# A four-layer decoder trunk: order edges behind the newest weight parts, read-backs used two stages later, and smaller pieces of side work

## The chip, the cores and the metric

The kernel runs on one core of one Trainium2 chip. Times are device microseconds (us) of a run of the whole program; lower is better. On the core, TensorE (PE) multiplies, ScalarE (ACT), VectorE (DVE) and GpSimd (POOL) work on rows, and SyncE (SP) issues transfers. Each engine works through its own instructions in order. POOL, SP and, twice, ACT also issue DMA transfers.

## What is computed

A decoder trunk with 256 positions, width 2048 and four layers in fp32. The layers' mixers are latent attention (MLA), sparse attention with an indexer and top-k (DSA), sliding-window attention with sinks, and latent attention again. Each layer also attends to a memory of 256 rows with four heads, and gates all heads. Cut to what matters:

```python
def reference(x, mem, ...):
    mem_n = _rmsnorm(mem, mem_norm)
    for i in range(DEPTH):                       # 4
        h = _rmsnorm(x, norm_in[i])
        self_out, mq, gate = <mixer i>(h, ...)   # h @ w_in, then attention: 2048 wide
        mem_out = _memory_attention(mq, mem_n @ w_mem_kv[i])      # 1024 wide
        y = jnp.concatenate([self_out, mem_out], axis=-1) * jax.nn.silu(gate)
        x = x + y @ w_out[i]
    return _rmsnorm(x, final_norm)
```

## The kernel before

**The stream of weights.** Nearly all arithmetic is activations times weights, and every weight is read once. SP loads a stage of weights, two slices of 128 rows by 512 columns (512 KB, tile `wr`, WR = 4 buffers, `stage`). fp32 is kept by splitting each number into two parts of a shorter type (fp32r): per slice, `parts_of` lets ACT copy `wr` to its high part `wh` (through `copy_act`, L75) and DVE subtract to get the low part `wl` (L84); each has WS = 4 buffers. `rows_by` (L381) then issues six matmuls of 128x512 per slice: for two halves of the positions, high by high, high by low and low by high. One slice with its copy, its subtraction and its six matmuls is called a *weight step* here. The results are `acc_q`, `acc_g` (the gate), `acc_mq` (queries to the memory), `acc_wo` (the output projection) and so on.

**Read-backs.** A result of `rows_by` has positions on partitions, and the next product needs features there. DVE turns it in blocks of 32 (`turn_blocks`, L284; tiles `et` and `th`), POOL writes that to DRAM (`put`, L299, `turned<-et`) and reads it back in the other layout with four transfers (`get`, L306, `fq<-turned`, `pT<-turned` and so on). That is a read-back. The tiles are `fa` (features of the low-rank queries, made into `cT` with a gain), `fq` (queries), `kn` (keys), `pT` (softmax weights), `gT` (the gate). Their consumers are: `row_parts` (the parts of fq, one 128x1024 copy on ACT and one subtraction on DVE), `exact_parts` (the same for kn and pT), in the grouped layers (DSA, window) the copies `qS<-fq`, in the latent layers `qrT<-fq` (rotary), `gained` for cT.

**Jobs and ticks.** `rows_by` calls `other_work` once per stage, that is every two weight steps; this is a *tick*. `after(n, job)` runs a job n ticks on. `features` puts a read-back's `get` BACK = 3 ticks behind its `put`, and its use USE = 9 ticks behind it. So the softmaxes (`weights`), the products with the values (`weighted`: `mo` L765, `o` L629 and L1197) and the gated outputs (`gated` L581, `write` L1207: DVE multiplies o with gT into `yt`, ACT and DVE split it into the parts of `y`) are written into the code between weight steps.

**What sets the order.** The code's order is not the last word: a scheduler puts each engine's instructions in an order by a timing model of its own, unless they are pinned (`keep_in_program_order`) or depend on each other. Weights loads are not pinned as a whole, so a consumer of a read-back can be placed earlier or later among the weight parts than it was written.

**Parts of a layer.** A layer's work runs in parts, in the order memory 0, self 0 to 3, memory 1: each part makes its queries, its gate and its attention, and while the next part's input products run, its `y` is finished; then `w_out` multiplies it (`acc_wo` reads `y`). `Part.finish` runs ticks without weights until y is written. In a grouped part `weights` runs as four jobs, two ticks apart, each with 4 quarter softmaxes, and `bm` (position biases, L1100) is loaded by POOL at the start of the part into a buffer that an earlier part holds. One `memset` per job (L1164) is POOL's.

**The last layer.** While it runs, `split_ahead` (L1332 to L1346) prepares the last part's output weights: POOL loads a piece of 128x256 into `hl` (2 buffers), ACT and DVE split it, and POOL writes it to DRAM (`sw`), so that the end can run without splitting. 16 pieces, ten half ticks each.

Of the kernel before, what the change touches and what calls it, by code (L numbers as in the profile page):

```python
# [15 lines left out]
P = 128  # L16
S = 256
# [10 lines left out]
PQ, AUX, WR, WS, PT, WARM = 3, 4, 4, 4, 4, 11  # L28
BACK, USE = 3, 9
# [17 lines left out]
def kernel(ctx: ExitStack, tc: tile.TileContext, a: dict, out: bass.AP,  # L47
# [23 lines left out]
    def part_tile(dt=F32R):  # L71
        return wk.tile([P, 512], dt, name="hl", tag="hl", bufs=2)
# [7 lines left out]
    pinned = []  # L80

    def split(hi, lo, src):
        copy_act(hi, src)
        nc.vector.tensor_sub(lo, src, f32(hi))  # L84

# [207 lines left out]
    def put(ets, d=None):  # L293

        u, n = len(ets), ets[0].shape[-1] // 4
        if d is None:
            d = dr.tile([u, 4, 32, 4, n], F32, name="turned", tag=f"turned{u * n}", bufs=6)
        for t, et in enumerate(ets):
            nc.gpsimd.dma_start(d[t].rearrange("i p j n -> (i p) (j n)"), et)  # L299
        return d  # L300

    def get(dst, d, pin=None):

        n = d.shape[-1]
        for j in range(4):
            inst = nc.gpsimd.dma_start(dst[32 * j:32 * j + 32].rearrange("p (i n) -> p i n", n=n),  # L306
                                       d[:, :, :, j, :].rearrange("t i p n -> p (t i) n"))
            if pin is not None:
                pin(inst)
# [21 lines left out]
    def gained(dst, gcol, n=4):  # L331

        def use(t):
            for m in range(n):
# [3 lines left out]
                copy_act(hi, src, scale=g)  # L338
                nc.vector.scalar_tensor_tensor(lo, src, g, f32(hi), op0=OP.mult, op1=OP.subtract)
        return use  # L340

    def row_parts(t):
# [4 lines left out]
        copy_act(h4, src)  # L347
        nc.vector.tensor_sub(l4, src, f32(h4))
        return hi, lo

    def exact_parts(hi, lo):

        copy_act(hi, f32(lo))
        nc.vector.tensor_sub(lo, f32(lo), f32(hi))

    def parts_of(wr, c0, n):
        wh = wp.tile([P, 512], F32R, name="wh", tag="wh", bufs=WS)
        wl = wp.tile([P, 512], F32R, name="wl", tag="wl", bufs=WS)
        split(wh[:, :n], wl[:, :n], wr[:, c0:c0 + n])
        return wh, wl  # L360

    def rows_by(xt, kts, w, k0, cols, name, prepare=None, each=None, exact_first=False):
# [4 lines left out]
        for s in range(0, kts, ST):  # L367
# [3 lines left out]
            for k in range(m):  # L371
# [7 lines left out]
                for n_, (t, v, w_) in enumerate(seq):  # L379
                    later = [z for z in seq[n_ + 1:] if z[0] == t]  # L380
                    nc.tensor.matmul(acc[t][:, :n], q[:, v, (s + k) % 4, t * P:(t + 1) * P], w_[:, :n],  # L381
                                     start=s + k == 0 and v == 0 and w_ is wh,
                                     stop=s + k == kts - 1 and not later)
# [195 lines left out]
    def gated(y, o, gT, j):  # L579
        yt = tmp("yt")  # L580
        nc.vector.tensor_mul(yt.rearrange("p (m u c) -> p m u c", m=2, c=32),  # L581
                             o.rearrange("p (m u c) -> p m u c", m=2, c=32),
                             gT[:, :, j:j + 2, :].rearrange("p u m c -> p m u c"))
        y3 = yt.rearrange("p (a b) -> p a b", a=2)
        split(y[:, 0, j:j + 2, :], y[:, 1, j:j + 2, :], y3)
# [40 lines left out]
    def attend(o, v, pT):  # L626

        for n_, (l, r_) in enumerate(((v[0], pT[0]), (v[0], pT[1]), (v[1], pT[0]))):
            nc.tensor.matmul(o, l, r_, start=n_ == 0, stop=False)  # L629
# [59 lines left out]
    class Memory(Part):  # L689
        def __init__(self, nm, i, w, mq0, g0, part, behind):  # L690
# [8 lines left out]
            def keys():  # L699
# [6 lines left out]
                get(flat_of(self.k[:, 1]), mk[i][part], pin)  # L706
                after(USE - BACK, lambda: exact_parts(self.k[:, 0], self.k[:, 1]))
# [3 lines left out]
            def queries(t):  # L711
                self.q = row_parts(t)
                for h in range(2):
                    after(1 + 2 * h, lambda h=h: self.weights(h))
# [3 lines left out]
        def weights(self, h):  # L718
# [4 lines left out]
            for b in range(2):  # L723
# [3 lines left out]
                for m in (2 * h, 2 * h + 1):  # L727
                    qh, ql = (z[:, m, b * P:(b + 1) * P] for z in self.q)
                    for l, r in ((qh, k[:, 0, :, m, :]), (qh, k[:, 1, :, m, :]), (ql, k[:, 0, :, m, :])):
                        nc.tensor.matmul(sp[:, :S], l, r, start=n_ == 0, stop=n_ == 5)  # L730
# [17 lines left out]
            def back():  # L748
                pL = weights_tile()[:, :512]
                get(f32(pL), d)  # L750
                after(USE - BACK, lambda: self.weighted(h, pL))
            after(BACK, back)

        def weighted(self, h, pL):
# [5 lines left out]
            for j in range(2):  # L760
# [3 lines left out]
                for n_, (l, r_) in enumerate(seq):  # L764
                    nc.tensor.matmul(o[:, j * S:(j + 1) * S], l, r_, start=n_ == 0, stop=n_ == 5)  # L765
# [17 lines left out]
    class Latent:  # L783
# [62 lines left out]
        def rotary(self, g):  # L846
# [9 lines left out]
            def use(zs):  # L856
                self.qr = [act.tile([P, 4, S], F32R, name="qrT", tag="aux", bufs=AUX) for z in range(2)]
                for z in range(2):
                    for h, main, low in ((0, slice(0, 64), slice(64, P)), (1, slice(64, P), slice(0, 64))):
# [3 lines left out]
                        copy_act(hi, src)  # L863
                        nc.vector.tensor_sub(lo, src, f32(hi))  # L864
# [5 lines left out]
    class LatentPart(Part):  # L870
# [30 lines left out]
        def weights(self, h):  # L901
            k, kr, qr = self.k, self.of.kr, self.of.qr[self.g % 2]

            def score(b):
# [8 lines left out]
                for n_, (l, r_) in enumerate(seq):  # L913
                    nc.tensor.matmul(sp[:, :S], l, r_, start=n_ == 0, stop=n_ == len(seq) - 1)  # L914
# [3 lines left out]
            def back():  # L918
                pT = weights_tile()
                get(f32(pT)[:, :384], d)  # L920
                after(USE - BACK, lambda: self.weighted(h, pT))
# [15 lines left out]
    class Grouped:  # L937
# [39 lines left out]
        def dup(self, dst, src, n):  # L977

            s3 = src.rearrange("p (g d) -> p g d", g=n)
            for g0 in range(0, n, 2):  # L980
                m = min(2, n - g0)
                hl = part_tile()[:].rearrange("p (g v e d) -> p g v e d", g=2, v=2, e=2)
# [108 lines left out]
    class GroupedPart(Part):  # L1091
        def __init__(self, of, g):
            super().__init__()
            self.of, self.g, nm = of, g, of.nm
            self.bm = bm = act.tile([P, 8, S], F32, name="bm", tag="big3")
            tab = tabs[0 if of.sparse else 1][g]
            for v in range(2):
                for e in range(2):
                    at = 64 * v + 32 * e
                    nc.gpsimd.dma_start(  # L1100
                        bm[at:at + 32, :4],
                        bass.AP(tensor=tab.tensor,
                                offset=tab.offset + 4 * e * N_TAB + 63 + 32 * v * (8 * N_TAB - 1),
                                ap=[[8 * N_TAB - 1, 32], [N_TAB, 4], [1, S]]))
# [7 lines left out]
            def queries(t):  # L1112
                self.q = [act.tile([P, 2, 8, 2, 32], F32R, name="qS", tag="pq", bufs=PQ) for z in range(2)]
                for z in range(2):
                    for h, main, low in ((0, slice(0, 64), slice(64, P)), (1, slice(64, P), slice(0, 64))):
                        hi, lo = (self.q[z][rows, h].rearrange("p u j c -> p u (j c)") for rows in (main, low))
                        src = t[main, :, 2 * z:2 * z + 2, :].rearrange("p u j c -> p u (j c)")
                        copy_act(hi, src)
                        nc.vector.tensor_sub(lo, src, f32(hi))
# [4 lines left out]
                for n in range(4):  # L1124
                    after(1 + 2 * n, lambda n=n: self.weights(n // 2, n % 2))
# [3 lines left out]
        def weights(self, half, odd):  # L1129
            of, g, bm, q = self.of, self.g, self.bm, self.q  # L1130

            def score(r, k0, n):
                sp = misc("sp")
                qb = q[half][:, odd, 2 * r:2 * r + 2].rearrange("p v j c -> p (v j c)")
                nc.tensor.matmul(sp[:, :2 * n], qb, of.k[:, g, :, k0:k0 + n], start=True, stop=True)
# [17 lines left out]
            if of.sparse:  # L1153
                e2, e1 = bm[:, 4 + half * 2 + odd, :], ring(P)
                quarter_softmax(score, bias, ((0, 0, e2[:, 192:]), (1, 0, e1)), None)
                turn_blocks(et, 0, e1)
# [4 lines left out]
            else:  # L1161
                nsk = nsink[:, u0:u0 + 1]
                e0, e1 = ring(P), ring(P)
                nc.gpsimd.memset(e0[:, 64:], 0.0)  # L1164
                quarter_softmax(score, bias, ((0, 0, e0[:, :64]), (1, 0, e1)), nsk)
                turn_blocks(et, 0, e0)
                turn_blocks(et, 1, e1)
# [5 lines left out]
            def back():  # L1173
# [3 lines left out]
                if len(self.pTs) == 4:  # L1177
                    after(USE - BACK, self.weighted)
# [269 lines left out]
```

## Time and profile before

| | |
|---|---|
| median of 3 runs | 2557.74 us (2557.07 to 2557.97) |
| the profiled execution | 2558.04 us |
| its span (first to last instruction) | 2556.1 us |
| granted TensorE clock, mean over the span | 0.992 |
| busy time of PE, DVE, ACT, POOL | 2498.3, 1853.7, 1520.6, 569.1 us |

The page gives each engine's busy time, then groups of instructions by line and tile with their count, busy time, mean in ns, and the idle time of the engine just before them with what ended it ("24.9 <-DMA fq<-turned 24.8": 24.8 us of 24.9 ended when the read-back into fq landed). The list of waits gives, for an engine and what released it, total us, number and longest. The windows view gives for each stretch of time the length, then busy time and count for PE, PEld, DVE, ACT and POOL, then the granted clock (1 is full speed), the DMA share and GB/s.

### The profile page before, as it was taken

How to read it: one execution, taken by the hardware profiler on the slowest of the kernel's cores; microseconds unless marked ns; L12 is line 12 of the kernel's file. 1: busy time of each engine (PE TensorE's matmuls, PEld its weight loads, DVE VectorE, ACT ScalarE, POOL GpSimd, SP SyncE). 2: the span in 40 equal slices, each digit the busy share in tenths (PEclk: the TensorE clock that was granted, in tenths of full speed). 3: DMA queues.
4: the chain of work that ended last, by engine and by line, in shares of the span. 5: the costliest groups of instructions: out<-in, count | busy, mean ns of one | idle time of the engine just before them, and what ended most of it. 6: DMA issues, size and time to landing. Idle time of an engine off the chain costs nothing. (4 is left out here: it accounts for less than half of the span.)

```text
span 2556.1 us, 37640 instructions
## 1 busy us (share of the span) xinstructions
PE 2498.3 (98%) x11766; PEld 2070.6 (81%) x11766; DVE 1853.7 (73%) x3840; ACT 1520.6 (59%) x3107; POOL 569.1 (22%) x1078
## 2 busy tenths in 40 slices
PE   9999999999999999999999999999999999999998
PEld 7888887787787889887878788878779778888887
DVE  6556555676776687887887776888867567777677
ACT  6555555565565557665666565666656555566564
POOL 3000001133222310123322112222320123432240
PEclk9999999999999999999999999999999999999999
DMA  8787767898879776778878677877875789997994
GB/s 283 250 267 236 235 213 227 233 259 238 228 233 264 236 243 203 222 225 255 276 234 246 200 222 245 253 246 246 245 238 173 224 248 278 267 263 225 269 313 148
DMA packets 404633, 613.96 MB, mean 240 GB/s; under 512 B 80881, under 2 KB 182641, under 8 KB 403793
## 3 DMA queue, kind: packets, MB, share of 16 engines
q1 hardware_dynamic: 347360, 449.71, 58.4%
q0 software_dynamic: 56352, 160.87, 20.3%
q8 instruction: 93, 1.52, 0.2%
q14 instruction: 108, 0.88, 0.1%
q10 hardware_dynamic: 720, 0.98, 0.1%
HBM read 535.83 MB, written 81.89 MB: 242 GB/s over the span
## 5 line engine op out<-in xcount | busy, mean ns | idle before, releaser
L75 ACT ACTIVATE wh<-wr 128x512 fp32r<-128x512 f32 (+1 forms) x1712 | 1046.5, 620 | 774.5 <-DVE wl L84 308.4
L84 DVE TENSOR_TENSOR wl<-wr,wh 128x512 fp32r<-128x512 f32 (+1 forms) x1712 | 1137.8, 676 | 482.7 <-ACT wh L75 473.2
L381 PE MATMUL acc_g<-wh,xT 128*128 128x512 f32 x1536 | 490.6, 394 | 5.3 <-ACT wh L75 5.3
L381 PE MATMUL acc_wo<-wh,y 128*128 128x512 f32 x1504 | 478.5, 393 | 3.6 <-ACT wh L75 3.4
L381 PEld LDWEIGHTS acc_g<-wh,xT 128*128 128x128 f32 x1536 | 290.7, 189 | 67.3 <-ACT wh L75 9.2
L381 PEld LDWEIGHTS acc_wo<-wh,y 128*128 128x128 f32 x1504 | 283.9, 189 | 62.5 <-ACT wh L75 5.6
L381 PE MATMUL acc_g<-wl,xT 128*128 128x512 f32 x768 | 304.6, 397 | 9.1 <-DVE wl L84 8.8
L381 PE MATMUL acc_wo<-wl,y 128*128 128x512 f32 x752 | 296.3, 394 | 2.2 <-DVE wl L84 2.0
L306 POOL DMA_DIRECT2D pT<-turned x320 | 175.0, 554 | 254.2 <-DMA turned<-et 43.1
L299 POOL DMA_DIRECT2D turned<-et x136 | 76.0, 559 | 549.7 <-DVE et L284 482.0
L381 PEld LDWEIGHTS acc_g<-wl,xT 128*128 128x128 f32 x768 | 145.4, 189 | 45.2 <-DVE wl L84 16.1
L381 PEld LDWEIGHTS acc_wo<-wl,y 128*128 128x128 f32 x752 | 142.2, 189 | 32.1 <-DVE wl L84 4.8
L381 PE MATMUL acc_mq<-wh,xT 128*128 128x512 f32 x512 | 162.6, 391 | 0.0
L381 PE MATMUL acc_mk<-wh,mT 128*128 128x512 f32 x512 | 160.4, 392 | 2.2 <-ACT wh L75 2.2
L381 PE MATMUL acc_q<-wh,xT 128*128 128x512 f32 x512 | 159.9, 390 | 0.0
L381 PE MATMUL acc_mv<-wh,mT 128*128 128x512 f32 x512 | 156.4, 389 | 0.9 <-ACT wh L75 0.9
L381 PE MATMUL acc_cq<-wh,xT 128*128 128x512 f32 x384 | 123.9, 402 | 6.4 <-ACT wh L75 6.4
L381 PE MATMUL acc_qn<-wh,cT 128*128 128x512 f32 x384 | 121.4, 392 | 3.5 <-ACT wh L75 3.2
L1367 DVE TENSOR_TENSOR xc<-xc,acc_wo 128x1024 f32<-128x1024 f32 x92 | 111.8, 1215 | 9.0 <-PE acc_wo L381 8.7
L381 PEld LDWEIGHTS acc_mk<-wh,mT 128*128 128x128 f32 x512 | 96.8, 189 | 22.8 <-ACT wh L75 2.6
L381 PEld LDWEIGHTS acc_mv<-wh,mT 128*128 128x128 f32 x512 | 96.0, 188 | 21.1 <-ACT wh L75 1.0
L381 PEld LDWEIGHTS acc_mq<-wh,xT 128*128 128x128 f32 x512 | 96.1, 188 | 19.8 <-ACT wh L75 0.7
(313 smaller groups left out, 3914.4 us busy)
## 6 DMA issues: line engine op xcount, KB each, us to landing
wr<-in_w_out_dram SPq DMA_DIRECT2D x188, 512.0 KB, 4.6
wr<-in_w_in_a_dram SPq DMA_DIRECT2D x176, 512.0 KB, 5.1
wr<-in_w_mem_kv_dram SPq DMA_DIRECT2D x125, 512.0 KB, 4.7
wr<-in_w_in_b_dram SPq DMA_DIRECT2D x116, 512.0 KB, 5.1
wr<-in_w_in_c_dram SPq DMA_DIRECT2D x104, 512.0 KB, 5.1
wr<-in_w_uq_dram SPq DMA_DIRECT2D x144, 256.0 KB, 5.3
turned<-et POOLq DMA_DIRECT2D x104, 256.0 KB, 4.4
wr<-in_w_ukv_dram SPq DMA_DIRECT2D x64, 256.0 KB, 6.0
```

Of the source, the lines that this page charges most:

```text
L75: inst = nc.scalar.activation(o, i, AF.Copy, scale=scale)
L84: nc.vector.tensor_sub(lo, src, f32(hi))
L299: nc.gpsimd.dma_start(d[t].rearrange("i p j n -> (i p) (j n)"), et)
L306: inst = nc.gpsimd.dma_start(dst[32 * j:32 * j + 32].rearrange("p (i n) -> p i n", n=n), d[:, :, :, j, :].rearrange("t i p n -> p (t i) n"))
L381: nc.tensor.matmul(acc[t][:, :n], q[:, v, (s + k) % 4, t * P:(t + 1) * P], w_[:, :n], start=s + k == 0 and v == 0 and w_ is wh, stop=s + k ...
L1367: nc.vector.tensor_add(xs, xs, acc)
```

## The change

It does nine things. No arithmetic is left out and none is added.

1. **Edges.** `weight_op` remembers per engine the newest weight part (ACT, DVE), the newest last matmul of a weight step (PE) and the newest `put` (POOL). `late` adds an edge without a semaphore from it to an instruction: the scheduler may not place that instruction ahead of it on its engine. `late` is applied to the consumers of read-backs (cT, fq, qS, qrT, kn, pT), to the first matmul of each score and of each product with values, to `yt` and the parts of y, and to the gets on POOL.
2. **Ticks.** BACK 3 to 4, USE 9 to 11; a new WAIT = 11 for the softmax weights; the memory's keys are still split 6 ticks behind their read, which USE - BACK no longer gives.
3. **WR** 4 to 5.
4. **Halves.** `row_parts` and the `qS` copies run in two halves, one tick apart; fq's copies become 128x512.
5. **Softmaxes** of a grouped part in eight jobs, one tick apart, in place of four. In a memory part 0 the second pair of heads is two ticks behind the first, in part 1 one tick.
6. **bm** is loaded 11 ticks later (`biases`).
7. **The memset** of e0 goes from POOL to DVE.
8. **`dup`** takes its tile `hl` from the ring of `tmp`.
9. **`split_ahead`** runs 32 pieces of 128x128 in place of 16 of 128x256, five half ticks each, through two buffers of half the size.

The diff, cut to its core:

```diff
-PQ, AUX, WR, WS, PT, WARM = 3, 4, 4, 4, 4, 11
-BACK, USE = 3, 9
+PQ, AUX, WR, WS, PT, WARM = 3, 4, 5, 4, 4, 11
+BACK, USE, WAIT = 4, 11, 11
...
+    newest = {}
+    def weight_op(inst):
+        newest[inst.ins.engine] = inst.ins
+    def late(inst):
+        behind = newest.get(inst.ins.engine)
+        if behind is not None:
+            tc.add_manual_dep(inst.ins, behind.name,
+                              mybir.DependencyInfo(mybir.DependencyClass.NoSync, mybir.DependencyReason.DATA),
+                              reason="behind the newest weights")
+    def late_copy(o, i, scale=1.0):
+        late(nc.scalar.activation(o, i, AF.Copy, scale=scale))
+    def late_split(hi, lo, src):
+        late_copy(hi, src)
+        late(nc.vector.tensor_sub(lo, src, f32(hi)))
...
     def put(ets, d=None):
-            nc.gpsimd.dma_start(d[t].rearrange("i p j n -> (i p) (j n)"), et)
+            weight_op(nc.gpsimd.dma_start(d[t].rearrange("i p j n -> (i p) (j n)"), et))
-    def get(dst, d, pin=None):
+    def get(dst, d):
-            if pin is not None:
-                pin(inst)
+            late(inst)
...
     def row_parts(t):
-        copy_act(h4, src)
-        nc.vector.tensor_sub(l4, src, f32(h4))
+        def half(m):
+            late_split(h4[:, m:m + 2], l4[:, m:m + 2], src[:, m:m + 2])
+        half(0)
+        after(1, lambda: half(2))
...
     def parts_of(wr, c0, n):
-        split(wh[:, :n], wl[:, :n], wr[:, c0:c0 + n])
+        inst = nc.scalar.activation(wh[:, :n], wr[:, c0:c0 + n], AF.Copy)
+        if pinned:
+            tc.keep_in_program_order(inst)
+        weight_op(inst)
+        weight_op(nc.vector.tensor_sub(wl[:, :n], wr[:, c0:c0 + n], f32(wh)[:, :n]))
...
             def queries(t):
-                for n in range(4):
-                    after(1 + 2 * n, lambda n=n: self.weights(n // 2, n % 2))
+                parts(0)
+                after(1, lambda: parts(1))
+                for n in range(8):
+                    after(1 + n, lambda n=n: self.weights(n // 4, n // 2 % 2, n % 2))
...
-                    after(USE - BACK, self.weighted)
+                    after(WAIT - BACK, self.weighted)
...
         def write(self, os):
-                nc.vector.tensor_mul(yt.rearrange("p (j u c) -> p j u c", j=2, u=8),
+                late(nc.vector.tensor_mul(yt.rearrange("p (j u c) -> p j u c", j=2, u=8),
-                split(y[:, 0, j:j + 2, :], y[:, 1, j:j + 2, :], yt.rearrange("p (a b) -> p a b", a=2))
+                late_split(y[:, 0, j:j + 2, :], y[:, 1, j:j + 2, :], yt.rearrange("p (a b) -> p a b", a=2))
...
     def split_ahead(w, part):
-        for n in range(16):
+        for n in range(32):
-            for _ in range(4):
+            for _ in range(2):
                 yield True
-            pin(nc.gpsimd.dma_start(split_w[n // 4][:, n % 4], q))
-            for _ in range(6):
+            m, c0 = n // 2, n % 2 * P
+            pin(nc.gpsimd.dma_start(split_w[m // 4][:, m % 4, :, c0:c0 + P], q))
+            for _ in range(3):
                 yield True
```

How the orders of the engines move. In them a row is line, operation, output<-inputs and shape, "x4" a run of four. On ACT in the first layer, where the memory part's queries `fq` are split ahead of the first softmax: `wh<-wr` is the copy of one weight step, `cT` the last of the low-rank queries, `hz` and `th` the gate. Before:

```order
L75 ACTIVATE cT_3406<-fa,gvec 128x256 x4
L75 ACTIVATE wh<-wr 128x512 x7
L75 ACTIVATE kn<-kn 128x1024
L75 ACTIVATE wh<-wr 128x512 x8
L75 ACTIVATE fq<-fq 128x1024
L75 ACTIVATE wh<-wr 128x512 x7
L75 ACTIVATE hz<-acc_g,xh 128x512
```

After:

```order
L97 ACTIVATE cT_3406<-fa,gvec 128x256 x4
L377 ACTIVATE wh<-wr 128x512 x15
L73 ACTIVATE hz<-acc_g,xh 128x512
L377 ACTIVATE wh<-wr 128x512
L97 ACTIVATE fq<-fq 128x512
L594 ACTIVATE th<-hz 128x512
L73 ACTIVATE hz<-acc_g,xh 128x512
L377 ACTIVATE wh<-wr 128x512 x2
L97 ACTIVATE fq<-fq 128x512
```

fq's copy has moved from eight weight steps ahead of the gate's hz to one behind it, in two halves with two weight steps between them; kn has gone ahead of cT.

On PE in the DSA layer, at the end of its second self part: the product `o` of the softmax weights with the values, and what follows it. Before:

```order
L1197 MATMUL o_12300<-pT2_11897,vs_9935 64x128
L1197 MATMUL o_12300<-pT2_11997,vh_11340 64x128
L1197 MATMUL o_12300<-pT2_11897,vh_11340 64x128
L381 MATMUL acc_g_12297<-wh_12442,xT_9624 128x512
L381 MATMUL acc_g_12297<-wl_12443,xT_9624 128x512
```

After:

```order
L1237 MATMUL o_12407<-pT2_12028,vs_9947 64x128
L1237 MATMUL o_12407<-pT2_12128,vh_11311 64x128
L1237 MATMUL o_12407<-pT2_12028,vh_11311 64x128
L403 MATMUL acc_wo_12536<-wh_12539,y_12425 128x512
L403 MATMUL acc_wo_12536<-wl_12540,y_12425 128x512
```

The last matmuls of o were followed by the gate's products, and are followed by the output projection that reads the y made from this o.

On POOL in the last layer: the loads `hl` and writes `sw` of `split_ahead`, among the writes and reads of the read-backs. Before:

```order
L1346 DMA sw2_133<-hl_23061 128x512
L1332 DMA hl_23240<-in_w_out_dram 128x256
L306 DMA pT_23418<-turned_23298 32x4x96 x4
L299 DMA turned_23409<-et_23379 128x384
L1332 DMA hl_23446<-in_w_out_dram 128x256
L306 DMA pT_23515<-turned_23409 32x4x96 x4
L1346 DMA sw2_133<-hl_23240 128x512
```

After:

```order
L1373 DMA hl_22768<-in_w_out_dram 128x128
L1388 DMA sw1_132<-hl_22687 128x2x128
L1373 DMA hl_22850<-in_w_out_dram 128x128
L1388 DMA sw1_132<-hl_22768 128x2x128
L1373 DMA hl_22960<-in_w_out_dram 128x128
L1388 DMA sw1_132<-hl_22850 128x2x128
L1373 DMA hl_23009<-in_w_out_dram 128x128
L1388 DMA sw1_132<-hl_22960 128x2x128
```

Loads and writes of the pieces, which stood apart among the read-backs, stand in one run there.

Weight steps that stand on ACT's and DVE's orders between the transposition that fills a read-back's source and ACT's first use of it (smallest and median of each kind):

| read-back | before | after |
|---|---|---|
| fq (28) | 5, 9 | 7, 17 |
| fa (8) | 9, 10 | 10, 17 |
| kn (16), smallest only | 8 | 14 |
| pT (48) | 6, 13 | 9, 15 |

The orders hold 32 rows more on ACT, 48 more on DVE, 16 more on POOL; PE has the same number, and SP's order is the same row for row.

More of the change, by code (lines that the diff above doesn't have):

```diff
@@ L380, in rows_by @@
                     later = [z for z in seq[n_ + 1:] if z[0] == t]
-                    nc.tensor.matmul(acc[t][:, :n], q[:, v, (s + k) % 4, t * P:(t + 1) * P], w_[:, :n],
-                                     start=s + k == 0 and v == 0 and w_ is wh,
-                                     stop=s + k == kts - 1 and not later)
+                    inst = nc.tensor.matmul(acc[t][:, :n], q[:, v, (s + k) % 4, t * P:(t + 1) * P], w_[:, :n],
+                                            start=s + k == 0 and v == 0 and w_ is wh,
+                                            stop=s + k == kts - 1 and not later)
+                weight_op(inst)
         return pair
@@ L628, in attend @@
         for n_, (l, r_) in enumerate(((v[0], pT[0]), (v[0], pT[1]), (v[1], pT[0]))):
-            nc.tensor.matmul(o, l, r_, start=n_ == 0, stop=False)
+            inst = nc.tensor.matmul(o, l, r_, start=n_ == 0, stop=False)
+            if n_ == 0:
+                late(inst)
         nc.tensor.matmul(o[:, P:], v[2], pT[2], start=False, stop=True)
@@ L713, in queries @@
                 for h in range(2):
-                    after(1 + 2 * h, lambda h=h: self.weights(h))
+                    after(1 + (2 - part) * h, lambda h=h: self.weights(h))
             features(from_rows(acc), pq_tile, queries)
@@ L913, in score @@
                 for n_, (l, r_) in enumerate(seq):
-                    nc.tensor.matmul(sp[:, :S], l, r_, start=n_ == 0, stop=n_ == len(seq) - 1)
+                    inst = nc.tensor.matmul(sp[:, :S], l, r_, start=n_ == 0, stop=n_ == len(seq) - 1)
+                    if n_ == 0:
+                        late(inst)
                 return sp
@@ L1113, in queries, with parts @@
                 self.q = [act.tile([P, 2, 8, 2, 32], F32R, name="qS", tag="pq", bufs=PQ) for z in range(2)]
-                for z in range(2):
+                def parts(z):
                     for h, main, low in ((0, slice(0, 64), slice(64, P)), (1, slice(64, P), slice(0, 64))):
@@ L1134, in score @@
                 qb = q[half][:, odd, 2 * r:2 * r + 2].rearrange("p v j c -> p (v j c)")
[L1135 removed]
+                late(nc.tensor.matmul(sp[:, :2 * n], qb, of.k[:, g, :, k0:k0 + n], start=True, stop=True))
                 return sp
@@ L1153, in weights @@
             if of.sparse:
-                e2, e1 = bm[:, 4 + half * 2 + odd, :], ring(P)
-                quarter_softmax(score, bias, ((0, 0, e2[:, 192:]), (1, 0, e1)), None)
-                turn_blocks(et, 0, e1)
+                e2 = bm[:, 4 + half * 2 + odd, :]
+                if not second:
+                    e1 = ring(P)
+                    quarter_softmax(score, bias, ((0, 0, e2[:, 192:]), (1, 0, e1)), None)
+                    turn_blocks(et, 0, e1)
+                    return
                 e3 = ring(S)
@@ L1162, in weights @@
                 nsk = nsink[:, u0:u0 + 1]
[L1163 to L1167, printed above, removed]
+                if not second:
+                    e0, e1 = ring(P), ring(P)
+                    nc.vector.memset(e0[:, 64:], 0.0)
+                    quarter_softmax(score, bias, ((0, 0, e0[:, :64]), (1, 0, e1)), nsk)
+                    turn_blocks(et, 0, e0)
+                    turn_blocks(et, 1, e1)
+                    return
                 e2 = bm[:, 4 + 2 * odd:6 + 2 * odd, :].rearrange("p a b -> p (a b)")
```

76 lines of the change are left out of this document (39 added, 37 removed).

## The prediction

> **What bounds the kernel now.** I read the page's busy times first, then the chain of waits in order of time, the list of waits, a timeline of one stall, and last the windows view over every stall of that kind.
>
> ```profile
> span 2556.1 us, 37640 instructions
> PE 2498.3 (98%) x11766; PEld 2070.6 (81%) x11766; DVE 1853.7 (73%) x3840; ACT 1520.6 (59%) x3107; POOL 569.1 (22%) x1078
> 2516.12 20.88 PE acc_wo L381 x92
> ```
>
> TensorE (PE) is the bound: its 2498.3 us leave 57.8 us of the span idle. In its densest piece, the third row (start, length, count, from the chain), 92 matmuls take 20.88 us, 0.227 us each, so one weight step of six matmuls is 1.36 us. The change takes no matmul away, so only PE's interruptions can shrink. What interrupts it starts on ScalarE (ACT); the list gives total us, times, longest:
>
> ```profile
> ACT fq L75 <- DMA fq<-turned: 38.8, 12, 6.2
> ACT pT L75 <- DMA pT<-turned: 26.3, 20, 3.5
> ACT qS L75 <- DMA fq<-turned: 24.8, 11, 6.5
> ACT cT L75 <- DMA fa<-turned: 18.5, 6, 4.5
> ACT kn L75 <- DMA kn<-turned: 13.0, 4, 5.5
> ```
>
> ACT stands 121.4 us in front of read-backs that have not landed. It works in order, so the weight parts (wh) behind them are late too. With four wh buffers ACT can be four steps, 5.5 us, ahead; a wait of that length uses all of it up. Three rows of one such place:
>
> ```profile
> 498.96 1.06 ACT L75 ACTIVATE fq<-fq 128x1024 fp32r<-128x1024 f32 x1 [6.17 <-DMA fq<-turned]
> 499.92 1.66 ACT L75 ACTIVATE wh<-wr 128x512 fp32r<-128x512 f32 x3
> 500.07 1.18 PE L730 MATMUL msp<-kn,fq 128*128 128x256 f32 x7 [2.50 <-ACT fq L75]
> ```
>
> I put windows round all 22 places of PE loss that have such a wait on ACT in them or just ahead. Shown are the six with the clock below full, and the sum (length, PE busy and count, then the others; PEclk is the granted clock):
>
> ```profile
> 408.00:421.00 13.00, 9.22 (x28) 6.71 (x27) 6.06 (x11) 5.94 (x14) 1.30 (x3) 0.74 0.53 164
> 826.00:835.00 9.00, 7.09 (x29) 5.55 (x28) 4.93 (x13) 4.41 (x9) 0.00 (x0) 0.81 0.85 256
> 1203.00:1217.00 14.00, 10.79 (x39) 7.85 (x38) 10.37 (x26) 7.62 (x17) 0.00 (x0) 0.88 0.35 98
> 1279.00:1291.00 12.00, 10.32 (x39) 7.85 (x39) 9.66 (x23) 6.88 (x15) 0.00 (x0) 0.86 0.36 111
> 1407.00:1425.00 18.00, 15.14 (x75) 11.04 (x74) 11.87 (x18) 9.11 (x15) 4.23 (x8) 0.81 0.67 216
> 2002.00:2016.00 14.00, 10.41 (x33) 7.81 (x33) 6.76 (x12) 6.45 (x15) 3.47 (x6) 0.76 0.56 183
> sum 207.00, PE 170.96 PEld 126.17 DVE 129.95 ACT 109.04 POOL 29.77; mean PE 7.77 PEld 5.73 DVE 5.91 ACT 4.96 POOL 1.35
> ```
>
> Idle there is 207.00 - 170.96 = 36.0 us. The lowered clock costs length times (1 - PEclk): 3.4 + 1.7 + 1.7 + 1.7 + 3.4 + 3.4 = 15.3 us. Together 51.3 us. It is a little more: a matmul's row is 0.39 us long while starts are 0.227 apart, so each gap hides 0.16 us; at about two gaps a place that is 7 us, in all 58.
>
> **Part by part. Read-backs later.** How much later stands in the orders: between the transposition that fills a read-back's source (DVE) and ACT's first use stand, by the median of each kind, 9 weight steps before and 17 after for fq (28 of them), 10 and 17 for fa, 13 and 15 for pT; pT's smallest goes from 6 to 9. What the way takes:
>
> ```profile
> turned<-et POOLq DMA_DIRECT2D x104, 256.0 KB, 4.4
> fq<-turned POOLq DMA_DIRECT2D x112, 128.0 KB, 5.2
> L306 POOL DMA_DIRECT2D fq<-turned x112 | 65.5, 591 | 121.3 <-DMA turned<-et 78.0 <-issue 41.1 <-DMA pT<-turned 1.6
> ```
>
> Write 4.4, four issues of 0.59, landing 5.2: 12.0 us, 8.8 steps, before any queueing on GpSimd (POOL). Nine steps leave nothing for queueing, seventeen leave 11 us. The queueing that the new edges add (a read stands behind the newest write, and that behind DVE) fits in it: counted from the newest write ahead in POOL's order, fq still keeps 10 or more steps in all but two of its 28, pT 8 or more. I take nine tenths of 58: **-52 us**, from -40 (a quarter stays) to -58. What is late next is ACT's own work, then the y chain below.
>
> **Smaller pieces, the fifth weight buffer.**
>
> ```profile
> L75 ACT ACTIVATE fq<-fq 128x1024 fp32r<-128x1024 f32 x16 | 16.9, 1055 | 38.8 <-DMA fq<-turned 38.8
> L75 ACT ACTIVATE qS<-fq 64x512 fp32r<-64x512 f32 x32 | 18.4, 622 | 24.9 <-DMA fq<-turned 24.8
> ACT wh L75 <- DMA wr<-in_w_in_a_dram: 22.7, 14, 3.0
> POOL bm L1100 <- PE acc_wo L381: 47.9, 1, 47.9
> ```
>
> fq's parts become halves, the softmaxes come in eight jobs, the memsets go from POOL to DVE: 32 instructions more on ACT and 48 on DVE, which are idle 41% and 27%. An ACT copy of 512 columns takes 0.62 us and one of 1024 takes 1.06, so the fixed part is about 0.2 us; 80 of these would be 16 us without that cover. I cost them at nothing. Nor do the bias loads (bm) cost anything: today POOL stands 47.9 us in front of one of them, with the read-backs queued behind; eleven ticks later that block shortens, and bm's first use is still 26 steps away. At four places ACT has the value copies (va) and four rotary copies (qrT) in one lump, and PE waits:
>
> ```profile
> sum 38.00, PE 33.20 PEld 25.08 DVE 28.11 ACT 27.70 POOL 11.19; mean PE 8.30 PEld 6.27 DVE 7.03 ACT 6.92 POOL 2.80
> ```
>
> That is 4.8 us in the windows 553:562, 734:742, 2147:2156 and 2321:2333. With use two stages later the lumps separate. The fifth wr buffer takes some of the 22.7 us for which ACT stands in front of wr loads (SP's own order is unchanged row for row), most of it already under PE: together **-4**, from 0 to -6.
>
> **The y chain, a new wait.** In the DSA and window layers a part's o now stands after the last gate matmul and directly ahead of acc_wo, which reads the y made from that o (second pair of orders); before, six steps lay between. PE has nothing to fill it. I find it at five places (two in the DSA layer, three in the window layer); at a sixth one step is left between. A chain of the same kind in the profile, under other work:
>
> ```profile
> 1737.34 0.39 PE L1197 MATMUL o<-pT,vh 128*64 128x128 f32 x4
> 1737.66 0.50 PE L381 MATMUL acc_g<-wl,xT 128*128 128x512 f32 x1
> 1738.50 0.68 DVE L1207 TENSOR_TENSOR yt<-o,gT 128x512 f32<-128x512 f32 x1
> 1739.71 0.62 ACT L75 ACTIVATE y<-yt 128x512 fp32r<-128x512 f32 x1
> 1740.45 0.68 DVE L84 TENSOR_TENSOR y<-yt,y 128x512 fp32r<-128x512 f32 x1
> ```
>
> PE is free at 1737.66; y's high part is there at 1740.33, its low part at 1741.13. The first acc_wo matmuls need the half written last: 2.67 us, and after two matmuls (0.45) the rest of 3.47 - 2.67: 3.0. In the new order qS copies and the gate's tanh stand in between on ACT, so up to 4.3 with two more such copies of 0.62. I take 3.6: **+18 us**, from +8 (1.5 each) to +25 (5 each). The clock: six of 22 places lost 15.3 us, so 0.7 us a place on average and 2.6 where it falls; 1 us each gives **+5**, from 3 to 13.
>
> On this the Trainium skill ("TensorE: Matmul & The Clock Gate", the part on the HAM clock gate) says that the clock halves after an idle window of about 3.4 us. By that rule waits of 3.6 us would seldom cost clock and the +5 would be 0, the time 2529; the trace differs, for the window 826:835 has 0.81 with 1.9 us of idle in all.
>
> **Splitting the last weights ahead.** split_ahead runs 32 pieces of half the width instead of 16, through two buffers.
>
> ```profile
> hl<-in_w_out_dram POOLq DMA_DIRECT2D x16, 128.0 KB, 5.0
> sw<-hl POOLq DMA_DIRECT2D x16, 256.0 KB, 6.8
> pT<-turned POOLq DMA_DIRECT2D x128, 48.0 KB, 4.1
> POOL hl L1332 <- DMA sw<-hl: 15.4, 4, 7.0
> ```
>
> A load needs its buffer's write landed, and on POOL it stands right behind that write; behind it stand other layers' reads. Halving a size does not halve its time (48 KB still 4.1), so I estimate 4.5 and 5.5 us: one turn of a buffer is 0.56 + 5.5 + 0.56 + 4.5 + 0.6 for the parts = 11.7 us, 5.9 a piece. In the new order the pieces stand 5.5 steps, 7.5 us, apart on average, but in two stretches some 13 pieces stand under 4 steps, 5 us, apart. ACT waits there, about 1 us a piece, half of it covered by its lead: **+7**, from 0 to +18. Last, at layer ends the memory part's second head is used three weight steps nearer its write: **+2**, from 0 to 6.
>
> **The sum.** -52 - 4 + 18 + 5 + 7 + 2 = -24. The profiled execution took 2558.04 us, 0.3 above the median of the three runs, which is nothing here: 2558.0 - 24 = **2534 us**.
>
> **Rivals.** First, the chains are shorter than their rows: DVE makes the first half while PE still does the second o, each place costs 1.5 us with no clock loss, the split pieces nothing: -52 - 4 + 8 + 2 = -46, **2512**. For it: 1.4 us of yt and y overlap o in the rows; against: the half needed first is written last. 19%.
>
> Second, the loss only moves: 6 us a chain (30), 13 of clock, 13 from the pieces: nothing is left, **2558**, with the case that the edges do not delay the uses (against it the orders): 14%.
>
> Third, slower. On ACT, qS stands ahead of the y that PE waits for, and qS's read-back is late as it is today: 6.5 us at its longest. Then each of five places costs 3.6 + 6.5 + 2.6 = 12.7 us, 64 in all: -56 + 64 + 7 + 2 = +17, **2575**. It decides from (56 - 9) / 5 = 9.4 us a place. For it: POOL must issue pT reads ahead of this fq; against: 15 steps stand between at four of the five (at the fifth ACT has exps and no qS), where 5 to 9 stood. 12%.
>
> **Chances.** The forecast 55%, its own range 2518 to 2549. Faster: 55 + 19 and 2 of the second's 14, 76%; same 11%, slower 1 and the third rival's 12, 13% ("same" is within 0.2%, 5 us, about what a measurement of this kernel can tell). The range, 2506 to 2562, leaves out the slower rival and the far end of the first.
>
> **What would show it.** Right: the five ACT rows fall from 121 to under 40 us, clock windows at 408, 1407 and 2002 go. New: PE acc_wo waiting for ACT y, about 3.6 us, at five places, and ACT hl waiting for its DMA after 2050 us. Wrong: ACT still waits over 80 us for read-backs (the steps were no cure), or PE idles over 8 us ahead of acc_wo.

## The result, and the profile after

The changed kernel took 2519.71 us against 2557.85 us before: ratio 0.985, 95% interval 0.9833 to 0.9867, 38 us less. Two later measurements, beside the experiments, gave 2525.72 against 2554.7 (0.9895, 0.9857 to 0.9933) and 2524.6 against 2556.7 (0.9883, 0.986 to 0.9905), 29 and 32 us less. The forecast was 24 us less.

From the page after, the span and the busy times:

```profile
span 2516.4 us, 37666 instructions
PE 2474.5 (98%) x11766; PEld 2065.5 (82%) x11766; DVE 1863.9 (74%) x3888; ACT 1537.2 (61%) x3139; POOL 588.6 (23%) x1094
```

PE still sets the time. It is idle for 41.9 us of the span in place of 57.8, and its busy time is 23.8 us less with the same matmuls. Of these 23.8, some 8.5 are clock: added up over windows of 8 us, the lowered clock cost 18.7 us before and 10.2 after. The list of waits after, and two rows of the groups (total, times, longest; in the groups the last number is the idle time before them):

```profile
ACT qS L97 <- DMA fq<-turned: 8.6, 7, 2.2
ACT cT L97 <- DMA fa<-turned: 1.2, 1, 1.2
ACT pT L97 <- DMA pT<-turned: 0.3, 1, 0.3
ACT hl L1383 <- DMA hl<-in_w_out_dram: 24.1, 11, 4.0
PE acc_wo L403 <- ACT y L97: 20.1, 5, 6.0
PE acc_wo L403 <- DVE y L101: 1.5, 2, 1.3
```

```profile
L97 ACT ACTIVATE fq<-fq 128x512 fp32r<-128x512 f32 x32 | 19.6, 618 | 0.0
L97 ACT ACTIVATE kn<-kn 128x1024 fp32r<-128x1024 f32 x16 | 16.8, 1051 | 0.3 <-DMA kn<-mk 0.3
```

The five rows of ACT in front of read-backs, 121.4 us before, are 10.1 us (fq and kn<-turned at nothing). A sixth row, the rotary copies qrT behind the read-back of fq, went the other way, from 1.0 to 5.4 us. A new row stands in their place on PE: five waits for y. Round those five places, and round the densest stretch of split pieces (last row), the windows view says (length; PE busy; the number third from the end is the granted clock):

```profile
1168.00:1182.00 14.00, 10.64 (x66) 7.78 (x65) 9.71 (x16) 8.32 (x14) 2.88 (x5) 1.00 0.73 219
1244.00:1258.00 14.00, 11.17 (x64) 8.28 (x63) 9.93 (x16) 8.33 (x14) 0.57 (x1) 0.88 0.62 185
1634.00:1662.00 28.00, 20.75 (x103) 16.07 (x102) 18.35 (x36) 13.84 (x26) 5.78 (x10) 0.88 0.67 196
1714.00:1738.00 24.00, 18.76 (x94) 14.32 (x93) 16.64 (x31) 12.56 (x22) 5.76 (x10) 0.86 0.66 195
1866.00:1878.00 12.00, 9.12 (x65) 6.77 (x64) 8.80 (x20) 6.82 (x17) 4.34 (x8) 1.00 0.71 245
2132.00:2156.00 24.00, 21.40 (x95) 17.33 (x94) 17.23 (x42) 13.31 (x30) 7.61 (x13) 0.93 0.72 209
```

Idle at the five is 3.36 + 2.83 + 7.25 + 5.24 + 2.88 = 21.6 us, and the clock takes 1.7 + 3.4 + 3.4 = 8.4: the y chain cost 30.0 us in this execution. In the stretch of the pieces the loss is 2.6 + 1.7 = 4.3 us. The profiled executions differ by 2558.04 - 2518.42 = 39.6 us, so all the rest of the change brought 39.6 + 30.0 + 4.3 = 74 us, if all the loss in these windows is put down to the change.

The costliest of the five places, on the timeline (start, length, engine; in brackets the idle time ahead and what ended it):

```profile
1638.66 0.42 PE L1237 MATMUL o<-pT,vh 128*64 128x128 f32 x4
1640.28 0.63 ACT L97 ACTIVATE y<-yt 128x512 fp32r<-128x512 f32 x1 [2.89 <-DVE yt L1247]
1640.40 0.42 PE L1237 MATMUL o<-pT,vh 128*64 128x128 f32 x4
1641.55 0.68 DVE L1247 TENSOR_TENSOR yt<-o,gT 128x512 f32<-128x512 f32 x1
1643.00 0.63 ACT L97 ACTIVATE qS<-fq 64x512 fp32r<-64x512 f32 x1 [2.09 <-DMA fq<-turned]
1643.53 0.67 ACT L73 ACTIVATE hz<-acc_g,xh 128x512 f32<-128x512 f32 x1
1644.23 0.63 ACT L594 ACTIVATE th<-hz 128x512 f32<-128x512 f32 x1
1644.77 0.67 ACT L73 ACTIVATE hz<-acc_g,xh 128x512 f32<-128x512 f32 x1
1645.46 0.63 ACT L97 ACTIVATE qS<-fq 64x512 fp32r<-64x512 f32 x1
1646.11 0.63 ACT L97 ACTIVATE y<-yt 128x512 fp32r<-128x512 f32 x1
1646.79 0.80 PE L403 MATMUL acc_wo<-wh,y 128*128 128x512 f32 x1 [5.98 <-ACT y L97]
```

The second half's yt is there at 1642.23, but ACT, in its order, first waits for a read-back that qS needs, then does two pieces of the gate, a tanh and another qS; only then comes the y that PE waits for, and acc_wo reads that half first.

### The profile page after: what moved, and what is told of

It reads as the page before. It is cut to its first block, busy times and chain, and to the rows that moved or that the text cites. A ratio compares the mean times of both kernels' runs of the same rounds, so it can differ in the third digit from the quotient of the medians.

```text
span 2516.4 us, 37666 instructions
## 1 busy us (share of the span) xinstructions
PE 2474.5 (98%) x11766; PEld 2065.5 (82%) x11766; DVE 1863.9 (74%) x3888; ACT 1537.2 (61%) x3139; POOL 588.6 (23%) x1094
## 5 line engine op out<-in xcount | busy, mean ns | idle before, releaser
L377 ACT ACTIVATE wh<-wr 128x512 fp32r<-128x512 f32 (+1 forms) x1712 | 1057.7, 622 | 819.0 <-DVE wl L381 361.3
L403 PE MATMUL acc_wo<-wh,y 128*128 128x512 f32 x1504 | 481.8, 395 | 24.0 <-ACT y L97 20.1
L403 PE MATMUL acc_g<-wh,xT 128*128 128x512 f32 x1536 | 480.9, 390 | 0.8 <-ACT wh L377 0.6
L403 PEld LDWEIGHTS acc_wo<-wh,y 128*128 128x128 f32 x1504 | 284.8, 190 | 86.6 <-ACT y L97 21.6
L323 POOL DMA_DIRECT2D pT<-turned x320 | 175.5, 554 | 40.1 <-DMA bm<-tab 10.6
```

Of the source, the lines that this page charges most:

```text
L377: inst = nc.scalar.activation(wh[:, :n], wr[:, c0:c0 + n], AF.Copy)
L403: inst = nc.tensor.matmul(acc[t][:, :n], q[:, v, (s + k) % 4, t * P:(t + 1) * P], w_[:, :n], start=s + k == 0 and v == 0 and w_ is wh, sto ...
```

## The experiments

They ran in three groups, each on a chip of its own beside the kernel before: 2548.96 us for the first four, 2554.7 for the next four, 2556.7 for the last. Ratios are to that. The first group has no run of the changed kernel.

**Four wr buffers.**

```diff
-PQ, AUX, WR, WS, PT, WARM = 3, 4, 5, 4, 4, 11
+PQ, AUX, WR, WS, PT, WARM = 3, 4, 4, 4, 4, 11
```

> The changed kernel with four wr buffers, as before the change, in place of five. Theory A (as forecast: the fifth buffer and the separated lumps are worth about 4 us, at most 6, since ACT's lead of four weight steps hides a late load): ACT's waits for wr landings come back to some 60 us, PE loses little by it, time 2520 to 2526. Rival B (the fifth buffer brought most of the gain that the forecast missed; ACT's waits for wr fell from 65 us in total to 4): 2532 to 2545, and PE is idle 10 us or more longer.

2534.08 us, ratio 0.9945 (0.9923 to 0.9968). By time this is rival B, by the waits theory A: the rows of ACT in front of wr add up to 64.8 us, as before the change, while PE's idle time is 2532.8 - 2483.2 = 49.6 us in place of 41.9. On its own the run does not settle it; two later runs, the fifth buffer without the rest and the edges alone, bear on it. The clock is part of it: added up over windows of 8 us it took 20.6 us here, and 10.2, 15.3 and 13.7 in the three profiled executions of the changed kernel.

**Old pieces, with four wr buffers.** The edit against the changed kernel, cut:

```diff
-PQ, AUX, WR, WS, PT, WARM = 3, 4, 5, 4, 4, 11
+PQ, AUX, WR, WS, PT, WARM = 3, 4, 4, 4, 4, 11
...
-            q = wk.tile([P, 2, P], F32R, name="hl", tag="hl", bufs=2)
+            q = wk.tile([P, 512], F32R, name="hl", tag="hl", bufs=2)[:].rearrange("p (v c) -> p v c", v=2)
...
-        for n in range(32):
+        for n in range(16):
```

> The kernel with four wr buffers (the old pieces and five buffers do not fit in memory together), and split_ahead in 16 pieces of 256 columns again. To be read against the run with four wr buffers alone. Theory A (small pieces cost PE about 5 us in the last layer): ACT's wait of 24 us in front of hl falls to under 6, and the time is 3 to 7 us less than with four buffers alone. Rival (the wait on ACT is covered by its lead): within 2 us of it.

2531.56 us, ratio 0.9921 (0.9893 to 0.9949), 2.5 us under the run with four buffers; the intervals overlap, so it is between the two theories and not settled. The row of ACT, of this kernel and then of that with four buffers:

```profile
ACT hl L1382 <- DMA hl<-in_w_out_dram: 5.5, 3, 3.1
```

```profile
ACT hl L1383 <- DMA hl<-in_w_out_dram: 18.6, 10, 7.1
```

ACT's wait is the pieces' doing; PE sees little of it.

**No edges.**

```diff
     def late(inst):
-        behind = newest.get(inst.ins.engine)
+        behind = None
```

> The changed kernel with every order edge left out; ticks, halves, five buffers and small pieces stay. In its order fq's first use stands 9 weight steps behind its transposition, as before the change (17 in the changed kernel), and two steps or more stand between the grouped parts' o and acc_wo. Theory A (it is the edges that make the uses late, and they also make the y chain): the five ACT rows in front of read-backs come back to 90 us or more, the waits of PE acc_wo for ACT y go; 50 of loss return and 30 go: about 2540, 2530 to 2550. Rival C (the ticks alone make the uses late enough): 2485 to 2500.

2543.14 us, ratio 0.9973 (0.9954 to 0.9991): theory A, rival C is out. Ticks, halves, five buffers and small pieces bring 5.8 us between them. That is less than theory A left: its 2540 was written beside a kernel before of 2558 us, and here that one takes 2548.96. The list of waits:

```profile
ACT fq L97 <- DMA fq<-turned: 36.7, 12, 5.3
ACT qS L97 <- DMA fq<-turned: 30.3, 10, 5.0
ACT cT L97 <- DMA fa<-turned: 23.6, 8, 4.8
ACT pT L97 <- DMA pT<-turned: 17.5, 14, 3.6
ACT kn L97 <- DMA kn<-turned: 9.4, 4, 3.5
```

The five rows are back at 117.5 us, and no row of PE acc_wo for y is left. The scheduler put the consumers where it had put them before; the later ticks did not stop it.

**Ticks back.**

```diff
-BACK, USE, WAIT = 4, 11, 11
+BACK, USE, WAIT = 3, 9, 9
```

> The changed kernel with BACK, USE and WAIT at 3, 9 and 9; the edges and all else stay. fq's first use stands 13 weight steps behind (median), 10 at the least. Theory A (the way of a read-back takes 12.0 us, 8.8 steps, and some queueing; the y chain is shortened at two or three of five places): 10 to 20 us of read-back waits on ACT, time 2510 to 2525, near the changed kernel. Rival D (the two further ticks carry most of the gain): over 60 us of read-back waits on ACT, 2535 to 2550.

2511.77 us, ratio 0.9847 (0.9811 to 0.9884): as good as the changed kernel, and rival D is out. The waits:

```profile
ACT qS L97 <- DMA fq<-turned: 13.1, 8, 4.0
ACT pT L97 <- DMA pT<-turned: 12.6, 11, 2.8
ACT fq L97 <- DMA fq<-turned: 7.1, 4, 3.5
ACT cT L97 <- DMA fa<-turned: 6.3, 4, 3.2
ACT kn L97 <- DMA kn<-turned: 2.2, 2, 1.3
PE acc_wo L403 <- ACT y L97: 6.8, 3, 5.1
```

41.3 us in front of read-backs, twice what I expected, and 6.8 us of waits for y in place of 20.1. So it is the edges that the time needs, and not the two further ticks: ACT still stands 41.3 us, but PE loses no more by it. What the two ticks add in cover they take back in the y chain.

**The changed kernel again.** (The same code.)

> The changed kernel as it is, run beside the others of this group so that they are compared on one chip. Both theories: ratio to before 0.985 within 0.004, since the first measurement gave that; the chip of the runs before this group was some 9 us faster for the kernel before and more uneven.

2525.72 us, ratio 0.9895 (0.9857 to 0.9933), spread from 2514.98 to 2537.52. This is just above what was expected (0.981 to 0.989).

**The half that is read first, written first.**

```diff
-            for half in (1, 0):
+            for half in (0, 1):
                 for l, i0, i1, c, start, stop in order:
...
-            for half in (1, 0):
+            for half in (0, 1):
                 j = half * 2
```

> The changed kernel with the two halves of a grouped part's output made in the order 0, 1 in place of 1, 0, in the products o and in the writing of y. acc_wo reads half 0 first. In the order the o of half 0 now stands 5 to 9 weight steps ahead of acc_wo at most places, that of half 1 directly ahead of it. Theory A (PE waits because the half that is read first is written last): the waits of PE acc_wo for y, 21.6 us in the changed kernel, fall below 8, and the time is 12 to 25 us less. Rival (PE only waits two weight steps later, for the second half, as the chain is longer than these 2.7 us): less than 6 us.

2511.76 us, ratio 0.9835 (0.9804 to 0.9866), 14.0 us less than the run above: theory A by the time. The intervals of the two overlap slightly, but four of the changed kernel's five executions are above all five of this one. The waits of PE acc_wo:

```profile
PE acc_wo L403 <- ACT y L97: 5.1, 3, 3.3
PE acc_wo L403 <- ACT hz L73: 5.2, 2, 2.9
```

The first row is below 8, as theory A says. The second is new: at two places of the window layer PE still stands 2.88 and 2.30 us between o and acc_wo, and what ends it there, by the profile, is the gate's hz on ACT. So four of the five places still have a wait, 10.1 us in all in place of 19.3 in the run above: half of it is gone.

**The fifth buffer, without the rest.**

```diff
-PQ, AUX, WR, WS, PT, WARM = 3, 4, 4, 4, 4, 11
+PQ, AUX, WR, WS, PT, WARM = 3, 4, 5, 4, 4, 11
...
-                hl = part_tile()[:].rearrange("p (g v e d) -> p g v e d", g=2, v=2, e=2)
+                hl = tmp("hl", dt=F32R)[:].rearrange("p (g v e d) -> p g v e d", g=2, v=2, e=2)
...
-        for n in range(16):
+        for n in range(32):
```

> The kernel before with a fifth wr buffer alone; to make room, split_ahead's small pieces and the tile for dup come with it. Edges, ticks, halves stay as before; the orders on PE, ACT and DVE are those of before but for the pieces. ACT waits 65 us in all for wr landings before. Theory A (forecast: most of that is under PE's and ACT's lead): ratio 0.997 to 1.000, up to 6 us less, some of it given back by the pieces. Rival B (a late load is what turns a read-back wait into a wait of PE; the buffer by itself brings much of what the forecast missed): ratio 0.990 to 0.994, 15 to 25 us less.

2553.1 us, ratio 0.9999 (0.9979 to 1.0019): theory A, rival B is out for the kernel before. Its waits for wr, all that are left, and the first of the read-backs:

```profile
ACT fq L75 <- DMA fq<-turned: 36.2, 12, 5.6
ACT wh L75 <- DMA wr<-in_w_mem_kv_dram: 3.4, 5, 1.3
ACT wh L75 <- DMA wr<-in_w_in_a_dram: 3.1, 3, 1.4
ACT wh L75 <- DMA wr<-in_w_out_dram: 2.6, 2, 1.8
```

Some 55 us of waiting for weights went from ACT, and the time did not change, as it should not if ACT was ahead.

**The edges alone.**

```diff
-PQ, AUX, WR, WS, PT, WARM = 3, 4, 5, 4, 4, 11
-BACK, USE, WAIT = 4, 11, 11
+PQ, AUX, WR, WS, PT, WARM = 3, 4, 4, 4, 4, 11
+BACK, USE, WAIT = 3, 9, 9
...
-        for n in range(32):
+        for n in range(16):
```

> The changed kernel with BACK, USE and WAIT at 3, 9, 9, four wr buffers and 16 pieces, as before the change: what is left of the change is the edges, the halves and the eight softmax jobs. Theory A (the edges carry the gain by themselves; the fifth buffer is worth a few us): 25 to 35 us less than before, ratio 0.986 to 0.990. Rival B (without the fifth buffer a good half is lost, as the run with four buffers suggests): 8 to 18 us less, ratio 0.993 to 0.997.

2518.06 us, ratio 0.9863 (0.9834 to 0.9893), 36.6 us less than before: theory A, and a little more than it expected. Besides the edges, the halves and the eight jobs this kernel keeps the small items 6 to 8 of the change (bm, memset, dup). With four buffers, old ticks and old pieces it is no worse than the changed kernel beside it (2525.72; the intervals overlap).

**The changed kernel a third time.** (The same code.)

> The changed kernel once more, as the measure for the three others of this group. Both theories: ratio to before 0.985 to 0.990, as in its two measurements so far.

2524.6 us, ratio 0.9883. Two of its windows, to be read against the first and the fifth of those above:

```profile
1165.00:1190.00 25.00, 22.29 (x106) 17.20 (x105) 18.36 (x33) 13.78 (x24) 6.88 (x12) 0.86 0.71 211
1864.00:1886.00 22.00, 19.11 (x107) 15.03 (x106) 14.86 (x29) 10.39 (x23) 8.40 (x15) 0.92 0.75 243
```

At the same two places, where the clock had stayed full, it now fell: 3.5 and 1.8 us more (over these two windows the first profile has 1.00). The waits there are 2.71 and 2.89 us, against 3.12 and 2.88 in the first profile.

**GpSimd's reads without their edges.**

```diff
             inst = nc.gpsimd.dma_start(dst[32 * j:32 * j + 32].rearrange("p (i n) -> p i n", n=n),
                                        d[:, :, :, j, :].rearrange("t i p n -> p (t i) n"))
-            late(inst)
```

> The changed kernel without the edges that order GpSimd's reads of read-backs behind its newest write; all other edges stay. In its order o then stands two or three weight steps ahead of acc_wo in the DSA layer (none in the changed kernel), and one or more at two of four places of the window layer. Theory A (these edges delay the reads, and with them o: without them the y chain is shorter): waits of PE acc_wo for y fall from 21 to under 14, time 4 to 12 us less than the changed kernel beside it. Rival (a read that stands ahead of a write holds that write up on GpSimd until its own source has landed, and the next read-back is late): the five rows of ACT in front of read-backs rise from 10 to 40 us or more, time 3 to 15 us more than the changed kernel.

2505.7 us, ratio 0.9808 (0.9783 to 0.9833), 18.9 us less than the changed kernel beside it: theory A, and more of it than I expected. Its waits:

```profile
ACT qS L97 <- DMA fq<-turned: 2.2, 2, 1.2
PE acc_wo L402 <- ACT y L97: 3.5, 1, 3.5
```

One wait for y is left of five, and those for read-backs are down as well. At the first place, on its timeline, gate matmuls stand behind o and cover the making of y:

```profile
1170.80 0.39 PE L1236 MATMUL o<-pT,vh 128*64 128x128 f32 x4
1171.12 0.50 PE L402 MATMUL acc_g<-wh,xT 128*128 128x512 f32 x1
1171.35 0.69 DVE L101 TENSOR_TENSOR y<-yt,y 128x512 fp32r<-128x512 f32 x1 [0.70 <-ACT y L97]
1171.96 0.68 DVE L1246 TENSOR_TENSOR yt<-o,gT 128x512 f32<-128x512 f32 x1
```

What the rival feared is there on GpSimd, and its price does not show in the time. The group of the pT reads, in this kernel, then in the changed one, then in the kernel before:

```profile
L323 POOL DMA_DIRECT2D pT<-turned x320 | 175.0, 553 | 286.8 <-DMA turned<-et 99.4 <-PE acc_wo L402 33.0 <-issue 31.1
```

```profile
L323 POOL DMA_DIRECT2D pT<-turned x320 | 175.5, 554 | 40.1 <-DMA bm<-tab 10.6
```

```profile
L306 POOL DMA_DIRECT2D pT<-turned x320 | 175.0, 554 | 254.2 <-DMA turned<-et 43.1
```

GpSimd stands 286.8 us in front of these reads in place of 40.1, about as long as in the kernel before. It is busy for 23% of the span and has the time. The gain is again idle time and clock: PE is idle 28.9 us in place of 41.2 beside it, and the clock, over windows of 8 us, took 5.1 us in place of 13.7.

**Ticks back and halves.** The two edits above together.

> The changed kernel with BACK, USE and WAIT at 3, 9, 9 and with the halves of a grouped part's output in the order 0, 1. In its order o of half 0 stands 7 to 15 steps ahead of acc_wo, that of half 1 one to five steps ahead at most places. Theory A (the two losses of the change, the y chain and the pieces, are separate from its gain, so taking the chain away adds up): waits of PE acc_wo for y under 4 us, ACT in front of read-backs about 45 us as with the ticks alone, ratio 0.978 to 0.983. Rival (the read-back waits of 45 us then decide): no better than the ticks alone, 0.985.

2505.44 us, ratio 0.981 (0.9785 to 0.9834), and no wait of PE acc_wo for y is left: theory A. The rival's 0.985 lies outside the interval, though the ticks alone, on another chip, have one that overlaps it. In front of the five kinds of read-back ACT stands 39.6 us. The pieces still make ACT wait:

```profile
ACT hl L1383 <- DMA hl<-in_w_out_dram: 27.8, 15, 4.3
```

**The edges alone, and halves.**

> The edges alone (ticks 3, 9, 9, four wr buffers, 16 pieces) with the halves in the order 0, 1. Against the run before it in this group it differs by the fifth buffer and the size of the pieces. Theory A (the buffer is worth a few us at most and the pieces cost about as much): within 5 us of that run, ratio 0.979 to 0.985. Rival (the fifth buffer is worth 10 us where the read-backs are on time): 8 us or more above it.

2509.1 us, ratio 0.982 (0.9794 to 0.9845), 3.7 us above the run before it, intervals overlapping: theory A. The fifth buffer and the small pieces together make no difference that shows; this pair cannot tell a gain of the one from a loss by the other.

This version, the one with ticks back and halves and the one without GpSimd's edges are the best that were run, 48 to 51 us under the kernel before. Leaving out GpSimd's edges was not tried together with the halves or the ticks.

## Why the prediction was right, point by point

**The sign and the mechanism** held. ACT's waits for read-backs were what interrupted PE: with edges they go and the time falls, without edges they stay and the time stays within 6 us. The clock windows at 408, 1407 and 2002 us are gone, as the prediction asks; up to 1244 us the clock is full, and its first fall is at the second wait for y. Edges are put on four engines, and only GpSimd's were taken out alone: which of ACT's, DVE's and PE's carry the gain is not shown. The size is partly luck. The gain and the y chain were both priced too low, by 20 and by 7 us in the profiled execution, and the two misses work against each other in the sum; 2519.71 is near the lower end of the forecast's own range, 2518 to 2549.

**Read-backs, -52, and the lumps and the buffer, -4.** In the profiled execution the sum of these and of all that is not the y chain or the pieces was -74, where the forecast has -54 (the 2 for the second heads included). In the third group it comes out nearer: the kernel without GpSimd's edges, which still has the pieces and one wait for y, is 51 us under before, where the forecast's terms without the y chain and its clock give 47. The first step at fault is "nine tenths of 58": the five rows fell by 111 of 121 us, and next to nothing was left. That is 6 of the 20 missing us. The whole span shows the rest. PE's idle time outside the five places and the stretch of pieces fell from 57.8 us to 41.9 - 21.6 - 2.6 = 17.7, 40.1 us less, where the forecast's rows have 36.0 + 4.8. The clock outside them fell from 18.7 us to nearly nothing, where the forecast's windows have 15.3, as they held only places with a wait of that kind beside a loss of PE. The remaining 15 us are busy time of PE that is not clock, where the forecast has 7 for the gaps hidden in the rows; what shortened it further was not measured.

**What makes the uses late.** I read the distance of 17 weight steps off the order and put it down to the change as a whole. The runs divide it: ticks and all else without edges bring 6 us, edges with the old ticks bring 37, and 13 steps are enough for the time, though ACT then still stands 41.3 us in front of read-backs. With the way at 8.8 steps, as worked out from the rows, that is what the sum of one read-back says; the further four steps were cover for queueing that I took to be needed.

**The fifth buffer.** That it is worth little was right for the kernel before (ratio 0.9999) and with the edges at the old ticks (3.7 us, with the pieces). The changed kernel with four buffers was slower than this allows (0.9945 beside 0.985 to 0.9895); the two were not run on one chip. In the profiled executions PE was idle 49.6 us in place of 41.2 to 42.0, and the clock took 20.6 us in place of 10.2 to 15.3. Why both were larger with four buffers stays open.

**The y chain, +18, and its clock, +5.** Five places, the right five, and the mechanism as described: o, yt, y and acc_wo in a row, with qS and tanh ahead of y on ACT. The price was too low in the profiled execution: 21.6 of idle and 8.4 of clock, 30 for 23. In the two later executions it was some 22 of idle and 14 of clock, 36. Taking it away returned less: 18.9 us (without GpSimd's edges, with one wait left) and 14.0 (halves, which leaves 10.1 us of waits). So 23 lies between what the chain cost where it stood and what its removal gave back. My 3.6 us a place averaged two kinds: 3 us in the DSA layer and at one place of the window layer, and 5 to 6 at the two other places of the window layer.

**The third rival**, qS late ahead of y, was therefore not a fancy: at four of the five places ACT stood in front of it just ahead of y, 2.25, 1.85, 2.09 and 1.48 us, so the 15 steps by which I argued against it were not enough. At 1646.79 it made 2.09 us of the 5.98. But the rival needed 9.4 us a place, and the five cost 30.0 / 5 = 6.0 on average; only this costliest one, with 7.25 of idle and 3.4 of clock, went over.

**The clock by the rule.** The Trainium skill ("TensorE: Matmul & The Clock Gate", the part on the HAM clock gate) also says that the window over which the activity is judged runs free, so that the same kernel measures differently from run to run. That fits the traces: the first of the five places kept a clock of 1.00 in one execution and had 0.86 over 25 us in another. The traces show no such window itself. Taken as a threshold for one wait, the 3.4 us would have made the +5 nothing; 8.4 us were lost, and some 14 in each of the two later executions.

**The pieces, +7.** ACT's wait came as forecast, 24.1 us; PE lost 4.3 us in the stretch shown, and the two pairs that differ in the pieces, 2.5 us one way and 3.7 the other (there the fifth buffer differs too), show no effect that can be told from none. **The second heads, +2,** did not appear as a row of their own. **Instructions added, 0:** nothing in the traces speaks against it.

**The first rival**, 2512, had the chain at 1.5 us a place. The time lay between it and the forecast, for another reason: the gain was larger, not the chain shorter.

## What to carry to other kernels

When a scheduler reorders the code, a consumer written later is not executed later: look in the order for where it ended up, and tie it behind the work that it must not overtake. Then follow the delayed chain to its end, since what is late everywhere at once will meet a place with nothing to cover it; there the order in which halves are produced (14 us here) or one edge too many (19 us) is worth as much as half the gain. A wait that vanishes from an engine with a lead is no gain by itself: 55 us of waiting for weights went from ACT and the time stayed.

## What the hardware showed that was not expected

A wait of PE of about 3 us costs clock in one execution and none in the next, at the same place of the same code (1.00 and 0.86 above); over the five places it took 8.4 us in the first profile, where the clock fell at three of them, and some 14 in each of the two later ones, where it fell at all five. The spread of the times does not show this: in the last group the changed kernel spread over 6.4 us, the kernel without GpSimd's edges over 5.4, and the kernel before, which has no such chain, over 16.0 (nine executions in place of five). GpSimd's reads issued far ahead of their data, 287 us of standing in all, went with the second lowest time that was run.
